# RWKV time mixing on one core: state steps moved by half a slot, the product with v moved into the next slot, zeros as fill on TensorE, and a rewritten drain

## The chip, the cores and the metric

The kernel runs on one core of a Trainium2 chip. The metric is the time of one execution on the device in microseconds; lower is better. The engines are called PE (TensorE, matrix multiply), DVE (VectorE), ACT (ScalarE), POOL (GpSimd) and SP (SyncE, which only issues transfers here).

## The reference

For each of 16 batches and 256 channels a recurrence runs over 2048 time steps. Its state is a weighted sum `aa` of values, a sum `bb` of weights and a running maximum `pp` that keeps the exponentials in range.

```python
for t in range(seq_len):
    ww = u + kk
    qq = np.maximum(pp, ww)
    e1 = np.exp(pp - qq)
    e2 = np.exp(ww - qq)
    output[b, t, :] = (e1 * aa + e2 * vv) / (e1 * bb + e2 + 1e-08)
    ww = pp - w + kk
    qq = np.maximum(ww, kk)
    e1 = np.exp(ww - qq)
    e2 = np.exp(kk - qq)
    aa = e1 * aa + e2 * vv
    bb = e1 * bb + e2
    pp = qq
```

Inputs and output are float32: k, v and the output have 33.55 MB each.

## The kernel before

Time is cut into 16 chunks of 128 steps (two halves of 64, one half in each half of the 128 partitions). A chunk of four batches is a tile of 128 partitions by 1024 numbers; there are 64 tiles for k, 64 for v and 64 for the output, 0.52 MB each. The main loop has one **slot** per tile (`n` from 0 to 63), and then 12 slots of drain. Four slots make one chunk of all 16 batches: a **period**; `n % 4` tells where in it a slot stands.

What happens to tile `n`, by the names in the code:

- `load_k`, `load_v`: six buffers each. k comes over SP's queue; v over SP's queue for the first 16 tiles and over POOL's queue after that.
- `round_k(n)` (L168) casts k to the format that PE multiplies, two slots ahead of use. DVE does it, except in slots with `n % 4` of 1 or 2 after slot 10, where POOL does.
- `logs(n)` (L196 and L200, the **exponents**): PE builds the decayed exponents, into two separate half tiles `xh` for the first nine tiles and into one tile `X` for the rest. Each has one buffer, so the exponents of tile n+1 wait for the exponentials of tile n.
- `exps(n)` (L206, L208): ACT takes the exponential and writes it into `EZR`, a ring of 12 tiles. In the first nine slots this goes in two halves.
- `cast_v(n)` (L215) casts v to bf16 into `vb`, which has two buffers; DVE or ACT does it for early tiles and POOL from tile 11 on. `times_v(n)` (L220) is the **product** with v on DVE, which stands at the end of slot n from slot 11 on.
- Ten slots later (`LAG`): `den` and `num` (L354), the sums over time by PE, each into a PSUM bank of its own with one buffer; `log_den` (L364, **logarithm**) and `invert` (L368, **inverse**) on ACT give 1/den as exp(-ln den); `mult` (L384, the **quotient**) on DVE multiplies and issues the store in three transfers on SP. The output tile `ot` has three buffers.
- `keep_going` (L360, the **fills**) multiplies zeros into the `den` tile, `DUM[n % 4]` times per slot. The logarithm of that tile waits for them.

Once per period the state is carried from chunk to chunk, in small **state steps**: `sums` (PE, 32 matmuls) and `copy_sums`, `turn` (PE) and `copy_turn` (tile `TS`), `state_logs` (ACT), `state_shift`, `state_frames` (a scan, L282) and `state_offsets` (DVE), a cap on POOL, `state_weights` (ACT, tile `G`), `state_chain` (the table product `TB`), `state_scan` (two scans, L309) and `state_spread` (DVE), `turn_back` (PE) and `inject`, which copies the carries and writes them over two ring rows of `EZR` by four small transfers, two on POOL's and two on SP's queue. They are queued in `later` by slot and by a name such as "frames"; the main loop takes each name up at its place.

Every instruction keeps the order in which the program writes it (`K`), so the main loop's text is the queue of each engine. Each engine takes its instructions in that order and waits where a tile isn't ready.

After tile 63's exponentials the exponent banks are freed and `den` and `num` get a second bank each (`drain`). There one of the three stores of a tile goes over POOL's queue, and the last tile's stores over SP and ACT.

Of the kernel before, what the change touches and what calls it, by code (L numbers as in the profile page):

```python
# [15 lines left out]
def kernel(  # L16
# [26 lines left out]
    DUM = (0, 4, 5, 3)  # L43
# [90 lines left out]
    def sum_matrices():  # L134
        OH = consts.tile([128, 56], BF16, tag="OH", name="OH")
        fill(OH, 0.0)
        for h in range(2):
            fill(OH[HS * h:HS * h + HS, 22 + h:23 + h], 1.0)
            fill(OH[HS * h:HS * h + 1, 30 + h:31 + h], 1.0)
        Sel = consts.tile([128, 3, 2, 2, 4, 2], F32, tag="Sel", name="Sel")  # L140
        fill(Sel, 0.0)
        for j, r in ((0, 64), (1, 0), (2, 8)):
            for h in range(2):
                select(Sel[:, j, h], NE, 1.0, -r - h, 1, [[-16, 2], [-2, 4], [-32, 2]])
        mats["OH"], mats["Sel"] = OH, Sel.rearrange("p a h x c i -> p (a h x c i)")
        Lx = matrix("Lx", F32)
        K(POOL.tensor_scalar(Lx, M1, -1.0, None, ALU.mult))
        for h in range(2):
            select(Lx, NE, 1.0, -(HS * h + HS - 1), 1, [[0, 128]])
        mats["Lx"] = Lx  # L150

# [71 lines left out]
    AS, D1, L1, A0, FR, _, BN = range(7)  # L223
    U_of = [consts.tile([128, 7, 32, 3], F32, tag=f"U{j}", name=f"U{j}") for j in range(2)]
    G_of = [consts.tile([128, 3, 32, 3], F32, tag=f"G{j}", name=f"G{j}") for j in range(2)]
# [5 lines left out]
    def state_start():  # L231
        for j in range(2):
            K(POOL.memset(CB_of[j], 0.0))
            K(POOL.memset(U_of[j][:, FR, :, 0:1], -BIG))
            K(POOL.memset(G_of[j][:, :, :, 0:1], 0.0))
        K(POOL.memset(U_of[0][:, D1, :, 0:1], -100.0))
        K(POOL.memset(U_of[0][:, L1, :, 0:1], 0.0))
        K(POOL.memset(TB_of[0][:, :, :, 0:1], 0.0))

    def sums(c):  # L240
        t = banks("num", "tot")[:, 0, 0:256]
# [16 lines left out]
    def turn(c):  # L258
        TS = banks("num", "TS")[:, 0, 0:192].rearrange("p (a x b m) -> p a x b m", a=6, x=2, b=2)
# [11 lines left out]
    def state_logs(c):  # L271
        K(SC.activation(U_of[c % 2][:, D1:D1 + 2, :, 1:3],
                        st[c, "TS"][:, 2:6, :].rearrange("p (a h) x -> p a x h", a=2), ACT.Ln))

# [9 lines left out]
    def state_offsets(c):  # L284
        U, nxt = U_of[c % 2], U_of[(c + 1) % 2]
        K(DVE.scalar_tensor_tensor(U[:, BN, :, 1:3], U[:, AS, :, 0:2], -1.0, U[:, FR, :, 1:3],
                                   op0=ALU.mult, op1=ALU.subtract))
        K(DVE.tensor_tensor(U[:, A0, :, 1:3], U[:, AS, :, 1:3], U[:, BN, :, 1:3], ALU.add))
        if drain:
            state_cap(c)  # L290
        if c + 1 < NST:
            K(POOL.tensor_copy(nxt[:, D1:D1 + 2, :, 0], U[:, AS:L1 + 1:2, :, 2]))  # L292

    def state_weights(c):
        K(SC.activation(G_of[c % 2][:, :, :, 1:3], U_of[c % 2][:, 0:7:3, :, 1:3], ACT.Exp, scale=-1.0))

    def state_cap(c):
        x = U_of[c % 2][:, BN, :, 1:3]
        K((DVE if drain else POOL).tensor_scalar(x, x, -CAP, None, ALU.max))
# [6 lines left out]
    def state_scan(c):  # L306
        G, TB = G_of[c % 2], TB_of[c % 2]
        for a in range(2):
            K(DVE.tensor_tensor_scan(AB[:, a].rearrange("p x h -> p (x h)"), G[:, 1].rearrange("p x h -> p (x h)"),  # L309
                                     TB[:, a].rearrange("p x h -> p (x h)"), 0.0, ALU.mult, ALU.add))  # L310

    def state_spread(c):
# [3 lines left out]
                         G[:, 2, :, 1:3].rearrange("p (b m) h -> p h b m", b=4).unsqueeze(1).broadcast_to([128, 2, 2, 4, 8])))  # L316
# [10 lines left out]

    def inject(c):
        if c == NST - 1:
            drain["carried"] = True  # L330
        cb = small.tile([128, 128], BF16, tag="cb", name="cb")
        K(DVE.tensor_copy(cb, st.pop((c, "CT"))))
# [29 lines left out]
    def log_den(n):  # L362
        rd = rpool.tile([128, 2, D], F32, tag="rd", name="rd")
# [11 lines left out]
    def mult(n):  # L375
# [4 lines left out]
        if last:  # L380
            for i in (1, 0):
                K(DVE.tensor_mul(oi[:, i], d[:, i], rd[:, i]))
        else:
            K(DVE.tensor_mul(oi, d, rd))  # L384
            K(SP.dma_start(out=dst[:, 0:2, :], in_=o[:, 0:2, :]))
        for h in range(2):
            K((POOL if drain and h and not last else SC if last and h else SP).dma_start(
                out=dst[HS * (1 - h):HS * (2 - h), 2:4, :], in_=o[HS * h:HS * h + HS, 2:4, :]))
        if last:
            for h in range(2):  # L390
                K((SP, SC)[h].dma_start(out=dst[HS * h:HS * h + HS, 0:2, :], in_=o[HS * h:HS * h + HS, 0:2, :]))
# [10 lines left out]
    for c in range(NST):  # L402
        s = 4 * c + 3
        if c == NST - 1:
            later[s, "last"] = [(sums, c), (copy_sums, c)]
            s -= 1
        for slot, where, f in ((s + 1, "sums", sums), (s + 1, "sums copy", copy_sums),
                               (s + 2, "turn", turn), (s + 2, "turn", copy_turn),
                               (s + 2, "logs", state_logs), (s + 2, "frames", state_shift),
                               (s + 2, "frames", state_frames), (s + 2, "frames", state_offsets),  # L410
# [119 lines left out]
```

## Time and profile before

| | |
|---|---|
| Runs (us) | 319.1, 316.5, 318.42; median 318.42 |
| Profiled execution | 319.99 us, of which the span is 318.3 us |
| Busy: PE, DVE, ACT, POOL | 254.9, 262.1, 259.7, 169.6 us (80, 82, 82, 53% of the span) |
| Bytes moved | 101.63 MB, mean 319 GB/s |
| Mean granted clock of PE | 0.922 |
| Transfers, issue to landing (median) | k 8.0 us, v on POOL's queue 7.2 us, stores 6.9 to 7.4 us, carries 5.5 to 5.9 us |

The page cuts the span into 40 slices of 7.96 us and gives tenths of busy time for each; PEclk is the clock that PE was granted, in tenths of full speed. A timeline row has start, duration (both us), engine, line, operation and tiles, and in brackets the idle time before it and what ended that. "SPq" and "POOLq" rows are transfers being issued. A row of the chain of waits has start, duration and what carried the time. A row of the groups has busy time in total and the mean duration of one in ns, then the idle time before them and its releaser.

Windows by stage, busy time in us of each engine (number of instructions in brackets left out):

| window, us | PE | DVE | ACT | POOL | PEclk | GB/s |
|---|---|---|---|---|---|---|
| 9.30 to 26.20 | 15.99 | 10.90 | 11.77 | 0.30 | 0.50 | 349 |
| 33.00 to 43.30 | 9.44 | 7.43 | 7.08 | 3.27 | 0.51 | 348 |
| 78.40 to 257.40 | 147.16 | 161.31 | 157.10 | 116.31 | 1.00 | 354 |
| 278.00 to 296.00 | 12.97 | 14.93 | 15.50 | 6.37 | 0.91 | 156 |
| 296.00 to 318.00 | 8.70 | 10.95 | 13.05 | 5.14 | 0.73 | 231 |

### The profile page before, as it was taken

Reading aid. Unit: us, or ns where it says so; the run is one execution under the profiler, and the core shown is the slowest. Engines: PE = TensorE matmul, PEld = TensorE weight load, DVE = VectorE, ACT = ScalarE, POOL = GpSimd, SP = SyncE. Lnnn points to the kernel's source line nnn. Section 1 sums busy time; section 2 is a strip of 40 time slices with the busy share of each in tenths; the row PEclk is TensorE's granted clock in tenths of the full one; section 3 lists DMA queues with packets and bytes.
Section 4 is the critical chain, followed back from the end, with each engine's and each line's share of the span. In section 5 each row is a group of like instructions: output and inputs, shape, how many; then the busy total and the mean of one; then the engine's idle time right before and its main releaser. Section 6 shows DMA issues by size and latency. Waiting matters only on the chain.

```text
span 318.3 us, 6417 instructions
## 1 busy us (share of the span) xinstructions
PE 254.9 (80%) x2324; PEld 127.7 (40%) x2351; DVE 262.1 (82%) x371; ACT 259.7 (82%) x244; POOL 169.6 (53%) x245
## 2 busy tenths in 40 slices
PE   7899887988788797788888797878788798975830
PEld 2334353444435344444434353434434354533310
DVE  4854768889898979989898889889898989898670
ACT  2665838988889889888889899888889889998880
POOL 5200136766574765766574765666574765432430
PEclk9556559999999999999999999999999999998695
DMA  7999999999999999999999999999999996646797
GB/s 191 356 348 349 348 337 347 344 385 297 321 348 359 358 296 334 382 373 390 361 374 305 381 332 379 339 346 360 357 373 338 373 352 202 169 120 169 206 273 203
DMA packets 86408, 101.63 MB, mean 319 GB/s; under 512 B 7068, under 2 KB 79848, under 8 KB 86376
## 3 DMA queue, kind: packets, MB, share of 16 engines
q1 hardware_dynamic: 77432, 73.91, 71.6%
q0 software_dynamic: 8640, 27.04, 25.1%
q8 instruction: 18, 0.29, 0.4%
q10 hardware_dynamic: 304, 0.27, 0.4%
q14 instruction: 14, 0.11, 0.1%
HBM read 67.12 MB, written 33.55 MB: 316 GB/s over the span
## 4 chain that ended last, share of the span: by engine, by line
DVE 27%; PE 24%; DMA 20%; ACT 15%; issue 7%; SPq 3%; POOL 1%; DVEq 0%; ACTq 0%; POOLq 0%
DMA out_dram<-ot 18%; DVE EZR L220 8%; ACT EZR L208 8%; DVE ot L384 7%; PE xh L200 6%; ACT rd L364 5%; PE X L200 5%; DVE AB L309 4%; PE xh L196 2%; PE num L354 2%; PE den L354 2%; PE TS L262 2%; ACT rd L368 2%; PE tot L247 2%; DMA kr<-in_k_dram 2%
## 5 line engine op out<-in xcount | busy, mean ns | idle before, releaser
L208 ACT ACTIVATE EZR<-X 128x2048 bf16<-128x2048 f32 x55 | 102.3, 1860 | 3.2 <-PE X L200 3.2
L220 DVE TENSOR_TENSOR EZR<-EZR,vb 128x2048 bf16<-128x2048 bf16 x64 | 88.9, 1389 | 8.3 <-ACT vb L213 6.0
L364 ACT ACTIVATE rd<-den 128x1024 f32<-128x1024 f32 x64 | 65.3, 1020 | 12.3 <-PE den L360 10.9
L215 POOL CAST vb<-vr 128x1024 bf16<-128x1024 f32 x53 | 55.0, 1038 | 36.2 <-DVE EZR L220 33.1
L368 ACT ACTIVATE rd<-rd 128x1024 f32<-128x1024 f32 x64 | 67.6, 1056 | 1.6
L384 DVE TENSOR_TENSOR ot<-num,rd 128x1024 f32<-128x1024 f32 x51 | 62.0, 1217 | 1.1 <-DMA out_dram<-ot 1.1
L68 POOL DMA_DIRECT2D vr<-in_v_dram x48 | 39.8, 829 | 15.1 <-POOL vb L215 10.4
L354 PE MATMUL num<-EZR,LN 64*64 64x512 bf16 x256 | 27.7, 403 | 22.9 <-DVE ot L384 19.1
L200 PE MATMUL X<-km,NLE 128*128 128x512 f32 x110 | 40.8, 452 | 0.8 <-POOL km L168 0.8
L360 PE MATMUL den<-Z 128*128 128x512 bf16 x138 | 36.6, 380 | 4.3 <-issue 4.3
L200 PE MATMUL X<-km,NLZ 128*128 128x512 f32 x110 | 35.0, 399 | 0.0
L196 PE MATMUL X<-WU,CO 32*128 32x512 bf16 x220 | 22.3, 390 | 15.1 <-ACT EZR L208 14.2
L292 POOL COPY U<-U 128x64 f32<-128x64 f32 x15 | 4.1, 276 | 52.5 <-DVE U L282 52.5
L168 DVE CAST km<-kr 128x1024 fp32r<-128x1024 f32 x39 | 30.2, 774 | 2.1 <-DMA kr<-in_k_dram 2.1
L196 PEld LDWEIGHTS <-CO 32*128 32x128 bf16 x256 | 11.4, 92 | 49.9 <-issue 47.3
L354 PE MATMUL den<-EZR,L 64*64 64x512 bf16 x256 | 28.2, 401 | 1.8 <-ACT rd L364 1.4
L354 PEld LDWEIGHTS <-LN 64*64 64x64 bf16 x256 | 13.2, 106 | 38.4 <-issue 33.8
L354 PE MATMUL num<-EZR,IdN 64*64 64x512 bf16 x256 | 27.6, 387 | 0.0
L354 PE MATMUL den<-EZR,Id 64*64 64x512 bf16 x256 | 27.2, 388 | 0.0
L309 DVE TENSOR_TENSOR_SCAN AB<-G,TB 128x96 f32<-128x96 f32 x32 | 26.5, 870 | 0.8
L168 POOL CAST km<-kr 128x1024 fp32r<-128x1024 f32 x25 | 26.2, 1049 | 0.1
L206 ACT ACTIVATE EZR<-xh 128x1024 bf16<-128x1024 f32 x18 | 18.2, 1019 | 8.4 <-PE xh L200 8.4
(76 smaller groups left out, 320.3 us busy)
## 6 DMA issues: line engine op xcount, KB each, us to landing
kr<-in_k_dram SPq DMA_DIRECT2D x64, 512.0 KB, 8.0
vr<-in_v_dram POOLq DMA_DIRECT2D x48, 512.0 KB, 7.2
out_dram<-ot SPq DMA_DIRECT2D x51, 256.0 KB, 7.4
out_dram<-ot SPq DMA_DIRECT2D x102, 128.0 KB, 6.9
vr<-in_v_dram SPq DMA_DIRECT2D x16, 512.0 KB, 8.8
out_dram<-od SPq DMA_DIRECT2D x12, 256.0 KB, 4.1
out_dram<-od SPq DMA_DIRECT2D x14, 128.0 KB, 3.7
out_dram<-od POOLq DMA_DIRECT2D x12, 128.0 KB, 3.4
```

Of the source, the lines that this page charges most:

```text
L68: K(q.dma_start(out=vr, in_=rows_of(v, n)))
L168: K(eng.tensor_copy(km, kr_of.pop(n)))
L196: K(PE.matmul(part_of(n, q)[:, i, :].rearrange("p (b d) -> p b d", b=2), CO[g:g + 32, :], WU[g:g + 32, :].unsqueeze(1).broadcast_to([32, 2 ...
L200: K(PE.matmul(part_of(n, q)[:, i, :], (NLE, NLZ)[q], km[:, i, :], start=False, stop=True, skip_group_check=True))
L208: K(SC.activation(ez(n)[:, 0:2], X_of[0], ACT.Exp))
L215: K(eng.tensor_copy(vb, vr_of.pop(n)))
L220: K(DVE.tensor_mul(ez(n)[:, 2:4], ez(n)[:, 0:2], vb.unsqueeze(1).broadcast_to([128, 2, 2, D])))
L309: K(DVE.tensor_tensor_scan(AB[:, a].rearrange("p x h -> p (x h)"), G[:, 1].rearrange("p x h -> p (x h)"), TB[:, a].rearrange("p x h -> p ( ...
L354: K(PE.matmul(d[x:x + HS, i, :], mats[m][r:r + HS, r:r + HS], ez(n)[r:r + HS, q, i, :], start=q == parts[0][1], stop=q == parts[1][1], til ...
L364: K(SC.activation(rd, DEN.pop(n), ACT.Ln, scale=RS))
L368: K(SC.activation(RD[n], RD[n], ACT.Exp, scale=-1.0))
L384: K(DVE.tensor_mul(oi, d, rd))
```

## The change

- **Start.** `state_start` sets its tables by memsets on DVE instead of POOL. In `sum_matrices` the order of two groups of set-up steps on POOL is exchanged.
- **Fills.** Slots 0 to 7 get three fills each, into a tile `pause` in the `den` bank. `DUM` goes from (0, 4, 5, 3) to (1, 1, 4, 4).
- **Product.** From slot 11 on the product of tile n moves from the end of slot n to the start of slot n+1, ahead of all else that DVE has there.
- **Casts of k** are all on DVE.
- **State steps.** Each moves later by about half a slot. `sums` and `turn` use the `den` bank instead of the `num` bank. The offsets become three steps (sum, a double difference, the cap), on POOL for chunks 2 to 14 and on DVE otherwise; the weights' exponential has 256 instead of 192 numbers per partition. The two scans become one of 192. The copy of the carries goes to ACT in most chunks.
- **Order in a slot.** The quotient comes after the product (and in slots with `n % 4` of 2 and 3 after the state steps); `num` stands ahead of `den` except where `n % 4` is 2.
- **Drain.** Slot 63 and the slots after it are written out by themselves (`ending`), with denominators two tiles ahead; `rd` takes `vr` buffers there; SP issues all stores, and the last tile's first half in one transfer.

```diff
-    DUM = (0, 4, 5, 3)
+    DUM = (1, 1, 4, 4)
...
     def state_start():
         for j in range(2):
-            K(POOL.memset(CB_of[j], 0.0))
+            K(DVE.memset(CB_of[j], 0.0))
...
     def sums(c):
-        t = banks("num", "tot")[:, 0, 0:256]
+        t = banks("den", "tot")[:, 0, 0:256]
...
+    def eng_of(c):
+        return DVE if c < 2 or c == NST - 1 else POOL
...
     def state_offsets(c):
-        U, nxt = U_of[c % 2], U_of[(c + 1) % 2]
-        K(DVE.scalar_tensor_tensor(U[:, BN, :, 1:3], U[:, AS, :, 0:2], -1.0, U[:, FR, :, 1:3],
-                                   op0=ALU.mult, op1=ALU.subtract))
-        K(DVE.tensor_tensor(U[:, A0, :, 1:3], U[:, AS, :, 1:3], U[:, BN, :, 1:3], ALU.add))
-        if drain:
-            state_cap(c)
+        U, nxt, e = U_of[c % 2], U_of[(c + 1) % 2], eng_of(c)
+        K(e.tensor_tensor(U[:, BC, :, 1:3], U[:, AS, :, 0:2], U[:, FR, :, 1:3], ALU.add))
+        K(e.tensor_tensor(U[:, A0:AA + 1:2, :, 1:3], U[:, AS, :, 1:3].unsqueeze(1).broadcast_to([128, 2, 32, 2]),
+                          U[:, BC, :, 1:3].unsqueeze(1).broadcast_to([128, 2, 32, 2]), ALU.subtract))
+        K(e.tensor_scalar(U[:, A2, :, 1:3], U[:, BC, :, 1:3], -1.0, -CAP, ALU.mult, ALU.max))
...
     def state_scan(c):
         G, TB = G_of[c % 2], TB_of[c % 2]
-        for a in range(2):
-            K(DVE.tensor_tensor_scan(AB[:, a].rearrange("p x h -> p (x h)"), G[:, 1].rearrange("p x h -> p (x h)"),
-                                     TB[:, a].rearrange("p x h -> p (x h)"), 0.0, ALU.mult, ALU.add))
+        K(DVE.tensor_tensor_scan(AB.rearrange("p a x h -> p (a x h)"), G[:, 1:3].rearrange("p a x h -> p (a x h)"),
+                                 TB.rearrange("p a x h -> p (a x h)"), 0.0, ALU.mult, ALU.add))
...
+    def copy_carries(c):
+        cb = small.tile([128, 128], BF16, tag="cb", name="cb")
+        if LAG < 4 * c + 7 < NP - 1:
+            K(SC.activation(cb, st.pop((c, "CT")), ACT.Copy))
+        else:
+            K(DVE.tensor_copy(cb, st.pop((c, "CT"))))
...
+    for n in range(NP):
+        q, kind = n - LAG, n % 4 if LAG < n < NP else -1
+        exps(n)
...
+        if LAG < n - 1 < NP - 1:
+            times_v(n - 1)
...
         if n + 1 < HALVES:
             logs(n + 1, (0,))
             logs(n + 1, (1,))
+            keep_going(psd.tile([128, 2, D], F32, tag="den", name="pause"), 3, True)
...
         if n >= LAG and n + 1 < NP:
             cast_v(n + 1, POOL)
+            if kind != 2:
+                next_v(n + 1)
+        if kind == 2:
+            small_work(n, "frames")
+        if kind == 3:
+            small_work(n, "chain")
+        if kind >= 0 and q >= 2:
+            mult(q - 2)
...
-        pooled = n > LAG and n % 4 in (1, 2)
-        if pooled and n + 2 < NP:
-            round_k(n + 2, POOL)
-            next_k(n + 2)
...
-        if LAG < n < NP:
-            times_v(n)
```

The steps of a chunk `c` (with `s = 4 * c + 3`), for all but the last chunk, by slot and place:

```diff
-        for slot, where, f in ((s + 1, "sums", sums), (s + 1, "sums copy", copy_sums),
-                               (s + 2, "turn", turn), (s + 2, "turn", copy_turn),
-                               (s + 2, "logs", state_logs), (s + 2, "frames", state_shift),
...
-                               (s + 3, "cap", state_cap), (s + 3, "weights", state_weights),
-                               (s + 3, "chain", state_chain),
...
+            plan = [(s + 1, "sums", sums), (s + 1, "sums", copy_sums), (s + 2, "turn", turn), (s + 2, "turn", copy_turn),
+                    (s + 3, "small", state_logs), (s + 3, "frames", state_shift), (s + 3, "frames", state_frames),
+                    (s + 3, "frames", state_offsets), ((s + 3, "late") if c > 1 else (s + 4, "small")) + (state_weights,),
+                    (s + 4, "chain", state_chain), (s + 4, "chain", state_scan), (s + 4, "chain", state_spread),
+                    (s + 4, "chain", state_keep), (s + 4, "turn back", turn_back), (s + 4, "back", copy_carries),
+                    (s + 4, "back", inject)]
```

## The prediction

> **What bounds the kernel now.** I read the page's strip of slices first, then the windows by stage, then the chain of waits and the timeline of each stage. A slot handles one pair tile of k and v; four slots are a period.
>
> ```profile
> PEclk9556559999999999999999999999999999998695
> DMA  7999999999999999999999999999999996646797
> ```
>
> Three stages show. From 9 to 47 us TensorE has half its clock nearly all the time; to 270 us all is steady; then the transfers thin out. Another row of the page gives 191 GB/s in the first slice and about 349 in the next four, where nearly everything is loads.
>
> The first stage, timeline and then chain of waits:
>
> ```profile
> 7.96 2.19 DVE L168 CAST km<-kr 128x1024 fp32r<-128x1024 f32 x1 [1.61 <-DMA kr<-in_k_dram]
> 8.00 0.53 POOL L233 MEMSET CB<- 128x512 bf16 x1
> ...
> 9.42 0.18 POOL L238 MEMSET TB<- 128x64 f32 x1
> 10.20 1.22 PE L200 MATMUL xh<-km,NLE 128*128 128x512 f32 x2 [1.24 <-DVE km L168]
> ```
>
> ```profile
> 18.72 1.15 PE xh L200 x2
> 19.88 0.54 PE xh L196 x2
> 20.41 1.15 PE xh L200 x2
> ```
>
> The cast of k tile 1 takes 2.19 us where its like takes 0.69: POOL's memsets hold it up to 9.6 us. TensorE stands still meanwhile, its clock falls at 9.3 us, and from there it is the chain without a gap, 2 x (0.54+1.15) = 3.38 us a slot.
>
> The steady stage, groups and then timeline:
>
> ```profile
> L208 ACT ACTIVATE EZR<-X 128x2048 bf16<-128x2048 f32 x55 | 102.3, 1860 | 3.2 <-PE X L200 3.2
> L364 ACT ACTIVATE rd<-den 128x1024 f32<-128x1024 f32 x64 | 65.3, 1020 | 12.3 <-PE den L360 10.9
> L368 ACT ACTIVATE rd<-rd 128x1024 f32<-128x1024 f32 x64 | 67.6, 1056 | 1.6
> ```
>
> ```profile
> 154.29 1.05 POOL L168 CAST km<-kr 128x1024 fp32r<-128x1024 f32 x1
> 154.31 2.12 DVE L220 TENSOR_TENSOR EZR<-EZR,vb 128x2048 bf16<-128x2048 bf16 x1
> 159.11 2.22 DVE L309 TENSOR_TENSOR_SCAN AB<-G,TB 128x96 f32<-128x96 f32 x2
> 160.06 1.05 POOL L168 CAST km<-kr 128x1024 fp32r<-128x1024 f32 x1
> ```
>
> Exponentials start at 78.40 (slot 17) and 257.44 us (slot 57): ten periods of 17.90 us. From start to start ScalarE needs 1.79 for exponentials, 1.05 for the logarithm (L364) and 0.97 for the inverse (L368), 3.81 a slot; with state logs 0.24 and weights 0.27 that is 15.8 a period, so 2.1 are stalls, of which 1.1 is the wait for the fills behind `den`. VectorE is as full (161.3 of those 179 us), but 2.5 us a period of it is blocking by POOL's casts of k: the product takes 2.12 for 1.21, the two scans 2.22 for 0.61.
>
> The drain:
>
> ```profile
> 308.82 1.48 SPq L385 DMA_DIRECT2D out_dram<-od  x1
> 310.34 0.60 SPq L387 DMA_DIRECT2D out_dram<-od  x1
> 311.04 1.45 SPq L385 DMA_DIRECT2D out_dram<-od  x1
> 312.53 1.91 SPq L387 DMA_DIRECT2D out_dram<-od  x2
> ```
>
> ScalarE does 11 pairs of 2.03 us; SyncE ends 4.4 us behind the last product at 310.7.
>
> **Start and clock.** The state's memsets move to VectorE behind that cast, which then ends at 8.65 instead of 10.15. They cost VectorE 1.2 us (two like the 0.27 of the Z memset, seven of about 0.1), done by 9.9, where the cast of v began anyway (10.07). So slot 1 starts 1.5 us sooner and TensorE keeps working through 9.3 us. Three fills of 128x512 per slot 0 to 7 cost 0.43 us each at half clock (ten in 4.45 us) and 0.22 at full (five in 1.25). With full clock a slot is 1.7 us of TensorE (the halves at 30 us: about 0.85) plus 0.7: no longer the bound. Slots 0 to 2 are then VectorE's, 0.60+1.15+0.62 = 2.4; slots 3 to 6 ScalarE's, 2 x 1.02 + 1.05 = 3.1; slots 7 and 8 about 2.8. From exponentials of slot 2 at 13.3: slot 3 15.6, slot 7 28.0, slot 9 33.6, with 0.8 for state work 34.4. Loads permit it: 1.5 MB in the first slice (191 GB/s), then 349 GB/s bring k tile 9, the 18th of 0.524 MB, at 30.7, so exponentials from 32.4. Before: 43.87. **-9.5 us.** Slots 9 and 10 at 3.9 instead of 4.4: **-1**. With the clock low all the way a slot is 3.38+1.28 = 4.66, and slot 9 begins at about 47.5: +3.6.
>
> Will the clock hold? I count 0.22 us of streaming for 512 columns, pairs on separate rows once. 29.6 to 33.0 us, after which it fell, has some 1.2 in 3.4: 35%. 143.0 to 146.4, the thinnest stretch I found in which it held, has 1.7 (exponents 1.3, carries 0.2, numerators 0.2): 50%. The new slot gives exponents 1.3 and fills 0.66 in 2.7 to 3.1 us: 63 to 73%. I take it as held. The Trainium skill, "TensorE: Matmul & The Clock Gate", Part 1, says that a sustained busy window of about 3.4 us releases the throttle and that it returns after an idle one. The two rises in this trace, at 29.6 and 46.7 us, lie five such windows apart, so the window agrees; but 9.3 to 26.2 us shows 15.99 of 16.90 us busy at clock 0.50, so plain busy time does not release it here. By the page alone the fills would add nothing to an engine that is 95% busy, and this term would be the 1.5 us of the start.
>
> **The steady period.** All k casts go to VectorE: +2 x 0.62. Off it go two offset steps (0.23+0.18), the cap was POOL's already, the carry copy (0.25), one scan (0.36 of 0.72; a scan twice as long was not run, so it saves 0 to 0.36). The 2.5 us of blocking by k casts go. What is late next: the product now opens the slot, POOL's cast of v starts as it ends (that is its release), and so falls on shift and scan in one slot and on the table product and scan in the next. A table product beside such a cast took 0.51 for 0.28 and ended 0.15 after it, so I count 0.9 of blocking for each. VectorE comes to 15.4+1.0, under ScalarE.
>
> ScalarE: 4 x 3.81 + 0.24 + weights 0.33 (256 elements for 192) + carry copy 0.2 = 16.0. Its waits, walked slot by slot:
>
> State slot (n%4 = 2). In the slot before, the copy of TS needs TensorE's exponents (1.91 to 3.36 after that slot's start) and TS itself (0.6); with the copy 0.28 and k's cast 0.60 VectorE is free at 4.9, which is about 1.0 into the state slot. Product to 2.2, POOL's cast to 3.2, the scan behind it to about 3.6. Three POOL steps follow, of which only the cap (0.37) was there before. One-input steps of this size took POOL 0.28 and 0.37, a copy 0.44; at 0.28 each the three take 0.85, with two inputs at double price 2.2; the nearest rows are 0.37 to 0.45, so 1.25. Weights start at 4.9, ScalarE was ready at 4.1 (1.79+0.24+1.05+0.97): 0.8 lost (0.4 to 1.75), and the next exponentials are queued behind. On POOL the load of v stands behind the offsets; it has about five slots until its use.
>
> Slots 3 and 0. In slot 3 VectorE does product (to 1.2 after the exponentials' start), table (1.5), waits for POOL's cast (2.6), scan and spread (3.3) and quotient (4.5); numerator, denominator and four fills follow to 6.5 while the logarithm could begin at 5.8: up to 0.7. If the scan is not blocked, that vanishes, and 0.2 comes up a slot later, where the denominator waits for the copy of the sums (now in its bank).
>
> The carries' four transfers follow ScalarE's copy, about 4.2 into slot 3, on POOL ahead of the next cast of v, on SyncE behind a k load. They landed in 5.5 to 5.9 us; the denominators that read them start some 11.5 after the same point. Before, the copy came at 4.8 (146.13 against 141.34), so that cover grows.
>
> So 17.0 to 17.5; I take 17.25. Ten periods save 6.5 us; with the POOL bounds 16.6 to 18.4, that is +5 to -13. **-6.5.**
>
> Transfers: a period moves 6.29 MB. The window 134 to 152 us ran 380 GB/s at share 1.07, which would allow 16.6; at 17.25 it is 365. Loads end near 268, 17 us ahead of the last product (285), and the gain eats this lead; I put **+1.5** for waits.
>
> **Drain.** The 11 pairs and two state steps are 23.0 of the 25.5 us from 283.95 to 309.40. The last carries still come late (logs a slot later), so I give 0.8 back. SyncE now has three issues a tile: 0.38+2x0.62 = 1.62 in quiet rows, under 2.03; but 2.8 and more by the late rows, which would be +8 over the tiles. If the transfers themselves set those rows, moving POOL's share costs nothing. I take +0.8. **0.** The order of setting up matrices, the rings for `rd` and fewer fills (10 a period for 12) I cost at nothing: POOL has them done by 8 us, `vr` buffers are free in the drain, and fills are cover only.
>
> Sum: 9.5+1+6.5-1.5 = 15.5 off 320.0 (the profiled run: span 318.3 and 1.7 around it; the median of the runs is 1.6 lower): 304.
>
> **Rivals.** *Clock not kept early* (17%): fills at 0.43 on the chain, 4.66 a slot. Against it the shares above, for it that even 95% busy did not raise it. +3.6-1-6.5 = -3.9: 316, 312 to 320.
> *POOL's offsets long* (12%): at 2.2 us ScalarE loses 1.75 and the period stays near 17.9, so only -9.5-1+1.5 is left: 311. For it: each step waits for the one before; against: the short rows.
> *SyncE bounds the drain* (10%): +8: 312. For it: SyncE has hardly a gap from 299.3 to 315.1; against it: quiet rows of 0.38 and 0.62.
> *No stalls* (8%): POOL's cast lets the scans through; the period is at the transfers' 16.6, 6.5 less than the forecast: 298.
> *Clock lost in the steady stage* (11%), the slower end: around the state slot TensorE waits for the quotient and for the late exponentials, and one stretch of 3.4 us holds exponents 1.3 and denominators 0.4: 1.7, the 50% that just held. Below that the next such stretch runs at half clock and each period pays 1.7 us: 13 x 1.7 = 22 on top: 326. Against it, the clock held through 240 us of such periods.
>
> **How the numbers follow.** Forecast 42%, 304, own range 297 to 310. For 8 in 10 I reach down past the case without stalls, by the 1.5 of waits and the two 0.8 of the drain, and up into the clock rival: 295 to 317. One per cent, what a measurement tells from no change, is 3.2 us: faster below 315.2 takes forecast, no stalls, offsets, SyncE and 4 of the clock's 17: 0.76. Within: 0.11, from the early clock. Slower: 0.11 and 0.02 of it, 0.13.
>
> **What would show it.** Right: TensorE's clock at 1.0 from 10 to 47 us and the first 128x2048 exponentials by 36; ScalarE waiting for POOL's offsets some 0.8 us a period; no k cast on POOL and scans of 1.0 to 1.6 us; period 17.0 to 17.5. Wrong: clock 0.5 in slots 1 to 8; a period at 17.9 with weights waiting 1.5; SyncE ending over 8 us after the last quotient; a clock dip in each period.

## The result, and the profile after

The changed kernel takes 328.19 us (median of four runs, 327.66 to 331.29); the kernel before, on the same chip, 317.70 (316.50 to 319.10). The ratio is 1.0344 (95% interval 1.0290 to 1.0399): slower, where the prediction said 304 and a range of 295 to 317. The profiled run is 328.14, its span 326.4. In the tables below, times are medians of all runs, and a ratio is formed without the runs that lie more than 1.5% above the kernel's fastest.

The page's strips of the changed kernel (40 equal slices: granted clock of TensorE, and transfers):

```profile
PEclk9999999979999999999999999999999999989875
DMA  6999999999999999999999999999999974436697
```

The half clock between 9 and 47 us is gone, as was forecast for the fills together with the moved memsets; every run that has the one has the other, so which of them did it is not shown. One slice near 70 us is at 0.7. It helped for a while. Start of the exponentials (L208) in both traces, and the difference:

| slot | before | after | difference |
|---|---|---|---|
| 9 | 43.87 | 37.20 | -6.7 |
| 10 | 48.85 | 40.69 | -8.2 |
| 17 | 78.40 | 75.80 | -2.6 |
| 57 | 257.44 | 259.57 | +2.1 |
| 63 | 282.07 | 287.58 | +5.5 |
| end of the last inverse | 309.40 | 315.54 | +6.1 |
| end of the span | 318.3 | 326.4 | +8.1 |

Read downwards, the gain of 8.2 shrinks by 5.6 between slots 10 and 17. Ten periods of 18.38 us for 17.90 cost 4.7, the last six slots 3.4, the drain 0.6, and the stores behind the last quotient 1.9 (9.5 us for 7.6).

Between slots 10 and 17, the chain of waits (start, duration, what; "DMA" is the time of a transfer):

```profile
46.06 0.29 DVE km L168
46.35 16.04 DMA vr<-in_v_dram
62.40 0.03 issue
62.42 0.02 POOLq L215
62.44 0.08 issue
62.52 1.04 POOL vb L215
63.56 0.72 POOL U L289
64.28 0.07 issue
64.35 1.06 POOL U L290
65.41 0.36 issue
65.77 0.44 POOL U L292
```

A load of v that SyncE issued at 46.35 us landed 16 us later; the transfers queued ahead of it are the likely reason. POOL's cast waited for it, and POOL's offset steps stand behind that cast: the state slot 14 took 7.5 us. One execution is not the whole picture here: in x7 and x11 below, whose programs are the same up to the drain, slot 14 took 5.9 and 6.5 us, and slot 17 began at 74.87 and 76.49.

A state slot of the steady stage, timeline (start, busy, engine, line; in brackets the idle time before and what ended it):

```profile
174.04 0.23 DVE L280 TENSOR_TENSOR U<-U 128x64 f32<-128x64 f32 x1
174.30 1.07 DVE L285 TENSOR_TENSOR_SCAN U<-U 128x96 f32<-128x96 f32 x1
175.30 1.19 DVE L393 TENSOR_TENSOR ot<-num,rd 128x1024 f32<-128x1024 f32 x1
175.46 0.31 POOL L289 TENSOR_TENSOR U<-U 128x64 f32<-128x64 f32 x1 [0.30 <-DVE U L285]
175.86 0.48 POOL L290 TENSOR_TENSOR U<-U 128x128 f32<-128x128 f32 x1
176.41 0.97 POOL L292 TENSOR_SCALAR U<-U 128x64 f32<-128x64 f32 x1
176.42 0.68 DVE L168 CAST km<-kr 128x1024 fp32r<-128x1024 f32 x1
177.41 0.43 ACT L297 ACTIVATE G<-U 128x256 f32<-128x256 f32 x1 [1.40 <-POOL U L292]
178.34 0.83 POOL L68 DMA_DIRECT2D vr<-in_v_dram  x1
178.58 2.08 DVE L306 TENSOR_TENSOR_SCAN AB<-G,TB 128x192 f32<-128x192 f32 x1
179.18 1.05 POOL L215 CAST vb<-vr 128x1024 bf16<-128x1024 f32 x1
```

Three things are to be seen. ScalarE stands still for 1.40 us before the weights (L297). The third offset step (L292) takes 0.97 us beside VectorE's cast of k; at 65.77 above it took 0.44, with nothing of VectorE's beside it. And the merged scan (L306) takes 2.08 us while POOL issues a load and casts; in the run x5 below it took 0.56. The third step's 0.95 to 0.97 us stands in all eleven steady periods of this trace. The waits of the whole run (us in total, times, longest):

```profile
ACT G L297 <- POOL U L292: 21.1, 13, 3.1
...
ACT rd L369 <- PE den L364: 8.9, 14, 1.7
```

That is 1.62 us a period for the weights (1.39 to 1.57 in the steady stage, 3.14 and 1.99 in slots 14 and 62), where the prediction had 0.8, and 0.64 for the logarithm behind the fills.

### The profile page after: what moved, and what is told of

Same layout as the page of the kernel before. It is cut to its first block, busy times and chain, and to the rows that moved or that the text cites. A ratio compares the mean times of both kernels' runs of the same rounds, so it can differ in the third digit from the quotient of the medians.

```text
span 326.4 us, 6396 instructions
## 1 busy us (share of the span) xinstructions
PE 251.1 (77%) x2348; PEld 123.3 (38%) x2348; DVE 268.2 (82%) x353; ACT 264.3 (81%) x256; POOL 157.8 (48%) x223
## 4 chain that ended last, share of the span: by engine, by line
DMA 24%; ACT 22%; PE 21%; DVE 18%; issue 6%; SPq 3%; POOL 2%; DVEq 0%; ACTq 0%; POOLq 0%
DMA out_dram<-ot 10%; ACT EZR L208 10%; DMA vr<-in_v_dram 8%; DVE ot L393 7%; DMA kr<-in_k_dram 6%; ACT rd L369 6%; PE X L200 4%; PE num L358 4%; PE den L364 4%; ACT rd L373 3%; PE tot L247 3%; PE den L358 3%; DVE EZR L220 3%; DVE AB L306 2%; DVE U L280 1%
## 5 line engine op out<-in xcount | busy, mean ns | idle before, releaser
L208 ACT ACTIVATE EZR<-X 128x2048 bf16<-128x2048 f32 x55 | 102.4, 1861 | 4.0 <-PE X L200 4.0
L220 DVE TENSOR_TENSOR EZR<-EZR,vb 128x2048 bf16<-128x2048 bf16 x64 | 78.5, 1227 | 3.9 <-ACT vb L213 2.7
L168 DVE CAST km<-kr 128x1024 fp32r<-128x1024 f32 x64 | 47.0, 734 | 2.6 <-DMA kr<-in_k_dram 2.6
L68 POOL DMA_DIRECT2D vr<-in_v_dram x48 | 37.7, 785 | 11.9 <-POOL vb L215 10.7
L364 PE MATMUL den<-Z 128*128 128x512 bf16 x138 | 39.2, 383 | 0.0
L341 POOL DMA_DIRECT2D EZR<-cb x36 | 20.5, 572 | 26.0 <-ACT cb L328 11.3
L358 PE MATMUL num<-EZR,IdN 64*64 64x512 bf16 x256 | 26.6, 392 | 0.0
L294 POOL COPY U<-U 128x64 f32<-128x64 f32 x15 | 11.6, 775 | 29.2 <-DVE U L285 28.4
L306 DVE TENSOR_TENSOR_SCAN AB<-G,TB 128x192 f32<-128x192 f32 x16 | 24.7, 1546 | 0.7
L364 PEld LDWEIGHTS <-Z 128*128 128x128 bf16 x162 | 12.8, 97 | 32.1 <-issue 24.5
L297 ACT ACTIVATE G<-U 128x256 f32<-128x256 f32 x16 | 6.8, 423 | 21.1 <-POOL U L292 21.1
```

Of the source, the lines that this page charges most:

```text
L68: K(q.dma_start(out=vr, in_=rows_of(v, n)))
L168: K(eng.tensor_copy(km, kr_of.pop(n)))
L208: K(SC.activation(ez(n)[:, 0:2], X_of[0], ACT.Exp))
L220: K(DVE.tensor_mul(ez(n)[:, 2:4], ez(n)[:, 0:2], vb.unsqueeze(1).broadcast_to([128, 2, 2, D])))
L358: K(PE.matmul(d[x:x + HS, i, :], mats[m][r:r + HS, r:r + HS], ez(n)[r:r + HS, q, i, :], start=q == parts[0][1], stop=q == parts[1][1], til ...
L364: K(PE.matmul(d[:, j % 2, :], Z[:, 0:128], Z, start=first, stop=True, skip_group_check=True))
```

## The experiments

| run | what | us (lowest to highest, runs) | ratio to before (95%) |
|---|---|---|---|
| changed kernel | | 328.19 (327.66 to 331.29, 4) | 1.0344 (1.0290 to 1.0399) |
| x1 | offset steps on VectorE | 326.00 (323.28 to 337.71, 4) | 1.0212 (1.0124 to 1.0300) |
| x2 | cast of v behind the first scan | 334.56 (332.79 to 337.47, 4) | 1.0518 (1.0432 to 1.0604) |
| x3 | cast of v behind both scans | 320.72 (317.14 to 324.32, 4) | none |
| x4 | ten early loads of v left out | 323.47 (1) | none |
| x5 | x1 and x3 | 320.99 (320.12 to 323.27, 10) | 1.0081 (1.0040 to 1.0122) |
| x6 | before with the new start | 317.50 (315.73 to 318.81, 10) | 0.9962 (0.9920 to 1.0004) |
| x7 | a store of each drain tile on POOL | 326.51 (324.57 to 327.28, 4) | 1.0221 (1.0154 to 1.0289) |
| x8 | x3 and x7 | 321.42 (314.90 to 325.76, 10) | 0.9993 (0.9911 to 1.0075) |
| x9 | half of the later loads of v left out | 327.08 (326.82 to 327.33, 2) | 1.0298 (1.0239 to 1.0357) |
| x10 | x3 and x9 | 311.07 (309.50 to 312.64, 2) | 0.9794 (0.9725 to 0.9863) |
| x11 | one store for a drain tile | 323.29 (322.49 to 324.63, 4) | 1.0183 (1.0139 to 1.0227) |
| x12 | x6, loads of v on POOL from tile 10 | 317.03 (315.48 to 318.78, 12) | 0.9987 (0.9959 to 1.0015) |
| x13 | third offset step on VectorE | 318.45 (316.46 to 323.94, 10) | 1.0005 (0.9967 to 1.0043) |
| x14 | x13, x3 and x7 | 318.59 (312.40 to 322.79, 12) | 0.9858 (0.9790 to 0.9926) |
| x15 | x13 and x7 | 317.66 (316.06 to 319.57, 12) | 0.9994 (0.9963 to 1.0024) |
| x16 | x15, third step ahead of the quotient | 323.09 (321.95 to 325.35, 6) | 1.0153 (1.0105 to 1.0200) |

**x1: the offset steps on VectorE.**

```diff
     def eng_of(c):
-        return DVE if c < 2 or c == NST - 1 else POOL
+        return DVE
```

> The changed kernel with the three offset steps on VectorE in every chunk. Theory A (the steady loss is ScalarE's weights behind POOL's three steps, 1.92 us from 175.46 to 177.38 in the state slot): the steps take about 0.7 us on VectorE, the weights' wait of 21.1 us in all falls under 6, the period from 18.4 to 17.2-17.7 us, the whole to 317-321 us. Theory B (VectorE or the transfers set the period and the weights' wait is only where it shows): the wait moves elsewhere, the period stays within 0.2 of 18.4 and the whole at 327-330.

The ratio fell from 1.034 to 1.021, less than the weights' wait alone would give. The profile was taken at a granted clock of 0.746 (337.71 us), so its lines can't be set beside the others, and where the rest went isn't read from it. Left open here; x5 and x13 take it up.

**x2 and x3: POOL's cast of v behind the scans.** In x2 the cast moves behind the state slot's shift, scan and offsets; in x3 also behind the table product, scan and spread of the slot after:

```diff
+        if kind == 2:
+            small_work(n, "frames")
+        if kind == 3:
+            small_work(n, "chain")
         if n >= LAG and n + 1 < NP:
             cast_v(n + 1, POOL)
             if kind != 2:
                 next_v(n + 1)
-        if kind == 2:
-            small_work(n, "frames")
-        if kind == 3:
-            small_work(n, "chain")
```

> The changed kernel with POOL's cast of v put behind the offsets in the state slot, so that shift, scan and offsets go first. Theory A: the scan falls from 1.07 to 0.36 us, the offsets begin 0.7 to 0.9 sooner, the weights' wait goes from 1.6 to 0.5-0.9 a period, the period to 17.5-17.8, the whole to 318-322 us. Theory B: no change beyond 0.2 us a period, 327-330.

> As the kernel before it, and POOL's cast of v also behind the table step in the next slot. If the cast alone blocks the long scan (2.08 us, 0.56 when nothing runs on POOL): scan 0.6, the quotient 1.4 us sooner, the wait of the logarithm for the fills in the slot after it (0.63) gone, period 16.8-17.2, whole 311-316. If the issue of a v load ahead of it blocks the scan too (178.34 to 179.17): scan about 1.0, period 17.0-17.5, 314-319. Theory B: 327-330.

x2 fell out the other way: the weights' wait went down to 8.7 us in all, but the time rose to 334.56. Its clock strip tells a part of why:

```profile
PEclk9999999979999899969969999999879699989975
```

TensorE lost its clock again and again in the steady stage: this is the rival "clock lost in the steady stage", in a neighbour of the changed kernel. There the spread (L311) took 2.04 us in ten of its sixteen turns, while POOL issued a load and cast, instead of 0.45, and ScalarE's copy of the carries waited 0.8 to 1.0 us in nine periods. Which of these starves TensorE enough isn't settled. The periods tell the two losses apart: four of the ten from 85.59 us on have the full clock and the long spread and take 18.4, as in the changed kernel, so the blocking had moved from the offsets to the spread; five have a mean clock of 0.84 to 0.91 and take 19.6 to 21.0; and the one whose spread took 0.45 (from 183.58 us) takes 16.99. x3 keeps the clock but for one slice, and five periods from 87.31 to 172.29 us are 17.0 each, inside the forecast. The second scan took neither of the two lengths expected: 1.27 us, beside the cast of v that had moved behind the offsets. Then its slots grow to 4.5 us. Windows before and after that point (PE, PEld, DVE, ACT and POOL busy us, then clock, DMA share and GB/s):

```profile
87.00:172.00 85.00, 73.89 (x732) 37.37 (x731) 77.24 (x96) 79.85 (x76) 56.42 (x76) 1.00 1.06 371
172.00:257.00 85.00, 72.18 (x710) 35.90 (x707) 73.84 (x92) 78.89 (x74) 50.66 (x71) 1.00 1.04 356
```

At 17.0 us a period asks for 370 GB/s, and in this run VectorE waits 12.2 us in all for an output buffer whose store has not landed. Whether the transfers are the cause is what x9 and x10 decide.

**x5: both remedies.**

> The changed kernel with the offset steps on VectorE (0.23 + 0.29 + 0.19 us a period more for it) and POOL's cast of v issued behind the scan of the frames in the state slot and behind the scan of the carries in the slot after. Nothing is left out of the computation. Theory A (the whole loss of the steady stage is the weights waiting for POOL's offset steps, plus blocked scans): the wait of the weights is under 0.3 us a period, both scans are at 0.36 and 0.56, periods about 17.0 until the transfers bind, time 312 to 317, and no faster than with the casts moved alone (320.7) by more than 5. Theory B (transfers of 6.29 MB a period at some 365 GB/s set 17.2 us whatever the engines do): periods start at 17.0 and come back to about 18 after 170 us, time 317 to 322, like the casts moved alone.

Theory A's waits came true (the weights' wait 2.4 us in all, scans of 0.36 and 0.56), its time did not: 320.99, periods of 17.5 but for two of 18.1 and 19.9. With the three steps in VectorE's queue the third is now the one that POOL's cast holds up (1.03 us for 0.19 in the steady periods), and the logarithm's wait for the fills grew to 22.1 us in all. The blocking moved rather than went away.

**x4: early loads left out.** Tiles 6 to 15 take the v of tile 5:

```diff
-            load_v(n + NBUF, SP if n + NBUF < FIRST else POOL)
+            if n + NBUF < FIRST:
+                vr_of[n + NBUF] = held[NBUF - 1]
+            else:
+                load_v(n + NBUF, POOL)
```

> The changed kernel, leaving out the loads of v for tiles 6 to 15, which use tile 5's v again (5.2 MB less to read). Theory C (the part of the early gain that is missing, 37.2 for 34.4 at slot 9 and 75.8 for about 69 at slot 17, went to transfers): slot 9 at 34-36, no wait for a v load at slot 14, slot 17 at 69-71.5, the whole 4-6 us shorter, period unchanged at 18.4. Theory D (engines set these slots): slot 9 within 0.7 of 37.2, slot 17 within 1 of 75.8.

Slot 9 starts at 37.23, as before the edit, so the loads of v from tile 6 on don't set that. Slot 17 starts at 73.17 instead of 75.80: some 2.6 of the 5.6 us that vanish between slots 10 and 17 go with those loads (1.7 to 3.3 beside the other executions of the same program, x7 and x11); the rest is there without them, in a state slot 14 that still takes 5.9 us (58.69 to 64.59), as state slots of the steady stage do (5.8).

**x6 and x12: the new start alone.** x6 is the kernel before with the memsets on VectorE, the selection matrix filled earlier, and

```diff
             logs(n + 1, (1,))
+            keep_going(psd.tile([128, 2, D], F32, tag="den", name="pause"), 3, True)
```

x12 adds `FIRST = 10` for 16.

> The kernel before with only the new start: the state's memsets on VectorE, the selection matrix filled earlier, and three fills of zeros in each of slots 0 to 7. Nothing is left out. If the early gain is real by itself: clock 1.0 from 10 us, slot 9's exponentials at 37 instead of 43.87, and the time 310 to 313 (-5 to -7). If the loads take it back (the wait for a load of v about slot 14, as in the changed kernel): slot 9 at 37, slot 17 at 74 to 76 instead of 78.4, time 314 to 316.

> The kernel before with the new start (317.5), and the loads of v from tile 10 on, instead of 16, issued by POOL, so that a store does not queue behind as many loads on SyncE's ring. Nothing is left out. If the early gain was lost only to the store that landed after 8.6 us behind queued loads: that wait is under 4 us, slot 17 at 73 to 75 instead of 77.5 and the time 312 to 315. If the sum of the bytes sets it: slot 17 at 77 again and 317.

x6 reaches slot 9 at 38.19, 5.7 us sooner, and slot 17 at 77.46, 0.9 sooner. Its chain of waits shows where the rest went:

```profile
58.96 1.93 SPq L385
60.89 0.05 issue
60.94 1.06 SPq L387
62.00 0.05 issue
62.05 8.60 DMA out_dram<-ot
70.69 0.04 issue
70.74 1.24 DVE ot L384
```

One of the first stores, queued behind the loads that run ahead, landed after 8.6 us, and the quotient waited for its buffer. Such a store stands at the same place in x3 (63.03, 7.03 us) and x13 (60.17, 9.28 us). In x12 it is gone from there, but slot 9 took 6.8 us and slot 17 starts at 76.83. Neither run is told from the kernel before. Slot 17 lies at 75.8 to 77.7 in the changed kernel, x3, x6, x12 and x13 whatever stalls on the way. This fits a place set by the bytes that have to be moved by then (348 GB/s with no gap from the second slice on). The soonest runs that move all of them are x16 (74.81) and x7 (74.87); those that move fewer come sooner still, x4 at 73.17, and x9 and x10 below at 73.44 and 72.11. That is no proof, and the engines' own stalls have a part in it.

**x9 and x10: transfers or engines in the steady stage.** Both leave out the loads of v for two of every four tiles from tile 19 on, x9 in the changed kernel and x10 in x3:

```diff
+            if n + NBUF > FIRST and n % 4 in (1, 2):
+                vr_of[n + NBUF] = held[n + NBUF - n % 4]
+            else:
-            load_v(n + NBUF, SP if n + NBUF < FIRST else POOL)
+                load_v(n + NBUF, SP if n + NBUF < FIRST else POOL)
```

> The changed kernel without the loads of v for two of every four tiles from tile 19 on (tiles 4m+3 and 4m+4 take the v of tile 4m+2): 5.24 MB a period for 6.29. It leaves that part of the input out, so its output is not the reference's. The loads that POOL issues in the state slot and the slot behind it stay. If engines alone set the changed kernel's steady period (weights behind POOL's offset steps): periods 18.2 to 18.4 as before (18.38), wait of the weights about 1.5 us a period. If transfers set it: 17.0 to 17.5.

> The same loads left out of the kernel with POOL's casts of v behind both scans (316.5 us of span, five periods of 17.0 and then 18 us). If its second half was held by transfers: 17.0 in all ten periods and the VectorE's wait for a store's buffer (12.2 us in all) under 3; span about 308 to 311. If something else sets in after 172 us: about 18 again there.

The pair decides. The changed kernel with a sixth of its bytes gone keeps its periods of 18.3 to 18.5, but for one of 19.5 (slots 21 and 57 start at 91.75 and 258.22: nine periods, 18.50 each) and its wait of 19.1 us for the weights: engines set it. x3 with the same bytes gone runs at 17.0 from end to end (98.77, 115.76, 132.75, 149.74, 166.73 and on to 251.63), its span is 307.8 for 316.5. Its windows:

```profile
87.00:172.00 85.00, 72.19 (x722) 37.17 (x731) 74.54 (x96) 80.02 (x76) 48.92 (x66) 1.00 0.98 315
172.00:257.00 85.00, 71.50 (x723) 37.41 (x730) 74.68 (x97) 79.88 (x76) 47.78 (x64) 1.00 0.94 302
```

ScalarE does as much in the second window as in the first, where x3 fell back, and the wait for output buffers is 1.9 us instead of 12.2. So the transfers, at share 1.06 and 371 GB/s, are the next bound right behind the engines, and cost 8.7 us of what x3 could give (the two spans).

**x13: the third step alone.** The step that scales and caps goes to VectorE, between the quotient and the cast of k:

```diff
         if kind >= 0 and q >= 2:
             mult(q - 2)
+        if kind == 2 and n // 4 - 1 > 1:
+            state_third(n // 4 - 1)
```

> The changed kernel with only the third of POOL's offset steps (scale and cap, 0.43 us alone, 0.97 beside VectorE's cast of k) put on VectorE, between the quotient and that cast; cast of v and order otherwise as changed. Nothing is left out. If VectorE's cast of k blocking that step is its share of the loss: the weights start some 0.6 us sooner, their wait falls from 1.5 to about 1.0 us a period, period 17.8, time 321 to 324. If the cast of v ahead of the steps holds them alone: wait 1.3 to 1.5, period 18.3, time 327 to 329.

It gave more than expected, 9.7 us by the medians. The state slot at 185.71 us, timeline:

```profile
189.25 0.31 POOL L289 TENSOR_TENSOR U<-U 128x64 f32<-128x64 f32 x1 [0.29 <-DVE U L285]
189.64 0.48 POOL L290 TENSOR_TENSOR U<-U 128x128 f32<-128x128 f32 x1
...
190.20 0.19 DVE L299 TENSOR_SCALAR U<-U 128x64 f32<-128x64 f32 x1
...
190.31 0.68 DVE L168 CAST km<-kr 128x1024 fp32r<-128x1024 f32 x1
...
190.48 0.43 ACT L302 ACTIVATE G<-U 128x256 f32<-128x256 f32 x1 [0.68 <-DVE U L299]
```

The weights start 0.10 us after the third step, and 4.77 us after the exponentials for 5.48 in the changed kernel. Their wait is 9.8 us in all (9.1 behind this step, 0.7 behind L290), 0.75 a period for 1.62; and the six periods from 103.20 to 208.35 are 17.52, for 18.38. The wait fell by 0.87 and these periods by 0.86; over all ten from slot 17 to 57 (76.08 to 252.48) a period is 17.64, 0.74 less, and VectorE's wait for output buffers has grown from 1.0 to 10.6 us. So in this order of steps the period follows the wait. It isn't the only term: x10 has the same wait (0.68) and periods of 17.0. The expectation had counted only the 0.54 of blocking, not the 0.43 of the step itself, which also left POOL's series.

**x16: the third step ahead of the quotient.**

```diff
+        if kind == 2 and n // 4 - 1 > 1:
+            state_third(n // 4 - 1)
         if kind >= 0 and q >= 2:
             mult(q - 2)
-        if kind == 2 and n // 4 - 1 > 1:
-            state_third(n // 4 - 1)
```

> The same with the third step ahead of the quotient in VectorE's queue. Nothing is left out. If the rest of the weights' wait (0.75 us a period) still sets the period: wait 0.3 to 0.4, periods of 17.1 to 17.2 where the transfers let them, time 312 to 315. If the transfers set it (at 17.5 they run at 359 GB/s): periods of 17.4 to 17.6 with longer waits for stores, time 316 to 318, as x15.

Neither happened. The wait for the weights fell to 0.45 us a period, and yet the periods came to 18.2 and the time to 323.09, 5.4 slower than x15. The chain of waits:

```profile
171.70 1.08 DVE U L285
...
172.86 0.32 POOL U L289
...
173.38 1.22 DVE ot L399
174.60 0.69 DVE km L168
175.29 1.13 DVE EZR L220
176.42 0.21 DVE TB L306
```

The chain now runs through VectorE: the third step waits for POOL's first (0.43 us at this place, 7.3 in all), and quotient, cast, product and table product queue behind it. The state slot is shorter (4.78 us), the one after it longer (4.98 for 3.98 in x13). VectorE is the other bound, half a microsecond away.

**x7 and x11: the drain's tail.** x7 gives POOL one of the three stores of each drain tile but the last, as before the change; x11 stores such a tile by one transfer of 512 KB, so the halves of two sequences land swapped:

```diff
-                K(SP.dma_start(
+                K((POOL if drain and h and not last else SP).dma_start(
```

```diff
+            if drain and not last:
+                if i == 0:
+                    K(SP.dma_start(out=dst, in_=o))
+                return
```

> The changed kernel with one of the three stores of each drain tile but the last issued by POOL again, as before the change. Nothing is left out. If SyncE's issuing sets the tail: the span ends 7.5 instead of 9.5 us after the last quotient, time 326 (-2). If the rate at which stores are written sets it (266 GB/s between 307 and 324 us): no change within 0.7, 328.

> The changed kernel with each drain tile but the last stored by one transfer of 512 KB instead of three (the rows of two sequences then land swapped in their halves; the bytes are the same). If SyncE's issuing sets the tail: the span ends about 7 us after the last quotient for 9.5, time 325 to 326. If the rate of writing sets it: 9 to 9.5, time 328.

The changed kernel's last issues:

```profile
313.91 1.27 SPq L390 DMA_DIRECT2D out_dram<-od  x2
315.27 0.54 SPq L388 DMA_DIRECT2D out_dram<-od  x1
315.57 1.29 DVE L396 TENSOR_TENSOR od<-num,rd 128x512 f32<-128x512 f32 x2 [0.77 <-ACT rd L373]
315.86 1.26 SPq L390 DMA_DIRECT2D out_dram<-od  x2
...
319.17 0.54 SPq L388 DMA_DIRECT2D out_dram<-od  x1
319.75 2.61 SPq L390 DMA_DIRECT2D out_dram<-od  x4
322.46 0.55 SPq L388 DMA_DIRECT2D out_dram<-od  x1
```

SyncE issues a tile every 1.95 us without a pause, and when the last quotient ends at 316.86 it still has some two tiles to go. Behind the last quotient the span ends after 9.5 us; in x7 after 7.9, in x11 after 5.1. With one transfer a tile the same bytes went at 340 GB/s in the next to last slice of the page, where the changed kernel shows 269. So issuing set the tail rather than the rate of writing: x7, with transfers of the same sizes, shows 1.6 us of it. x11 changes the size of the transfers as well as their number, so which of the two gave its further 2.8 us isn't told apart. By the ratios x11 is 1.6% under the changed kernel.

**x8, x14, x15: together.**

> The changed kernel with POOL's cast of v behind the scans (as in the run that gave 320.7) and the split stores of the drain. Nothing is left out. If the two effects add: 318 to 319 by theory SyncE, 320 to 321 if the rate of writing sets the tail.

> The third step on VectorE, POOL's casts of v behind both scans, and one store of each drain tile on POOL. Nothing is left out. If the engines' loss was the weights and the scans: no wait of the weights over 0.2 us, periods of 17.0 or less until transfers set in, both scans at 0.36 and 0.56 in most periods; the transfers then hold the body at about 17.5 on average: 315 to 319, at most 1% off the kernel before. If the removal of the wait lets the whole steady stage run at 17.0: 310 to 312.

> The third step on VectorE behind the quotient (318.45) and one store of each drain tile on POOL. Nothing is left out. If SyncE's issuing sets the tail it gains 1.5 to 2 there: 316.5 to 317, some 0.4% under the kernel before; if not, 318.4.

x8 gains nothing over x3. x14 scatters between 312.4 and 322.8; its ratio of 0.9858 rests on its two lowest runs of twelve, and its median of 318.59 is no better than x13's, so no gain is claimed. In its profiled run the quotient waited 23.0 us for stores, and the third step, queued behind the quotient, with it: 9.8 us of waiting for the weights are back, by way of the transfers. x15 is 317.66 beside 317.72 for the kernel before: the change mended in two places is no slower and no faster. No version that does the whole work is shown to beat the kernel before.

## The prediction, step by step

**The clock, right; the size of the start, too large.** The clock is full through the first slots and the exponentials of slot 9 came 6.7 us sooner, not 9.5; at 37.20 they missed the sign that was named, "by 36". Between 9.3 and 26.2 us TensorE was busy for 15.70 of 16.90 us at clock 1.00, where before it was 15.99 at 0.50, so the share of busy time doesn't tell the two states apart; whether the fills made the difference or the closing of the gap that the memsets had left stays open. Slot 3 began at 15.52, as reckoned (15.6); slots 3 to 6 took 14.3 us for 12.4, slots 7 and 8 took 7.4 for 6.4. The prediction had checked the loads of k alone, and ScalarE's cast of v tile 3 waited 0.64 us for its load, which landed at 18.07; the rest of the chain passes through work on TensorE that was taken as cover: three fills of a slot, 0.68 us, between two slots' exponents, and the first chunk's sums (1.06). Then the gain was lost: of 8.2 us at slot 10, 2.6 were left at slot 17. The prediction kept the whole 10.5 to the end, so this is its second largest miss (7.9 us), and its cause is shown only in part (x4, x6).

**The steady period, wrong, and this is the step that failed.** "At 0.28 each the three take 0.85, with two inputs at double price 2.2; the nearest rows are 0.37 to 0.45, so 1.25", and so "0.8 lost". The walk up to there was good: the first scan ended 3.44 us after the exponentials' start (reckoned: 3.6) and ScalarE was ready at 4.09 (4.1). The steps took 0.31, 0.48 and 0.97, with their gaps 1.92, and ScalarE lost 1.40 here and 1.62 on average. The period came to 18.38, the far end of the bounds that the prediction gave for POOL (16.6 to 18.4). The term was mis-sized because the rows it was taken from had no cast of k beside them, and the change itself put that cast on VectorE, right behind the quotient. The Trainium skill, "SBUF — State Buffer", section "Who interferes with whom", says that VectorE and GpSimd share a pair of ports as an exclusive lock, that copies, casts and `tensor_scalar` on VectorE can take it, and that the other engine then blocks for the whole instruction. The trace agrees: 0.97 us beside a cast of 0.68, 0.44 without; and the steps beside the quotient, which reads its numerator from PSUM, kept 0.31 and 0.48. x13 is the proof: with that step off POOL, and so neither blocked nor in POOL's series, the wait came to 0.75, the size that was forecast, six periods to 17.5, the upper end of the forecast, and the time fell by 9.7 us. Of the 11.3 us by which ten periods missed 17.25, 7.4 hang on this step (17.64 over the ten). The walk's other term came as reckoned: the logarithm behind the fills waited 0.64 for "up to 0.7". In x10, where the second scan ends 0.8 us sooner, the slot with `n % 4` of 0 takes 3.86 for 4.52 us and the next one 4.10 for 3.91, the 0.2 that was said to come up a slot later.

**What made the miss larger than the rival.** "POOL's offsets long" had the mechanism and nearly the size (1.75), and put the time at 311. It kept the early gain of 10.5 whole and the last six slots at no cost. But the last slots of the kernel before run at 3.84 us once loads thin out, while in the changed kernel the state slots there still take 5.8 and 6.4: +3.4.

**Transfers, +1.5, far too small for the schedule that was forecast.** x3 against x10: 8.7 us. In the changed kernel itself the term was not put to the test: without a sixth of the bytes (x9) its periods stay as they are. The prediction noted 380 GB/s in one window and took it as room; 371 GB/s is where five periods of 17.0 stood, and no kernel that moves all bytes held it through the steady stage. With x13 the steady term is nearly as forecast, and the time is still 318 and not 304.

**The drain.** The rival "SyncE bounds the drain" was right in kind, though its sign, "SyncE ending over 8 us after the last quotient", did not show: SyncE's last issue ended 6.2 us after it (4.4 before), and the span 9.5 (7.6). It was priced at 8 us in all; the tail cost 1.9 against the kernel before and 4.4 against one transfer a tile.

**Rivals that didn't happen here.** The clock held through the steady stage of the changed kernel, though x2 shows how near that was. The mean scans were 0.67 and 1.55 us, within the 1.0 to 1.6 that was named only for the second. The carries' transfers, whose cover was to grow, held TensorE up once, for 1.4 us in slot 10 (0.3 in all before). One scan for two, the rings and the order of setup show no wait that the kernel before didn't have.

## What to carry to other kernels

A step's price is that of its neighbours in the new order: list what the other engine runs at that moment, and when the change moves that work too, take no row in which it was elsewhere. Before adding up gains on engines, work out the rate of transfers that the faster schedule asks for, and give away all that lies above the rate that some long stretch of the trace has held. A gain at the start is only a gain if the queues behind it can move the bytes sooner.

## What the runs showed of the hardware

- A small step on GpSimd beside VectorE's cast of k took 0.97 us for 0.44; in slot 14 the first step took 0.74 beside that cast and the second 1.34 beside VectorE's product, whose inputs both lie in SBUF, for 0.31 and 0.48 beside the quotient.
- The scan of 192 on VectorE took 0.56 us alone, 1.27 beside a cast on GpSimd (x13) and 2.08 with the issue of a load ahead of that cast (178.34 to 179.17). An issue without a cast behind it did not slow it (0.56 at 68.53 us in the changed kernel), so why the issue ahead of a cast adds so much is open.
- One transfer of 512 KB a tile reached 340 GB/s in a slice of the drain, three transfers of 256, 128 and 128 KB 269; SyncE took 1.95 us to issue the three.
- A load queued at 46.35 us landed 16.04 us later, and stores at that stage 7.0 to 9.3 us after the end of their issue, against medians, from the issue, of 8.9 for such loads and 5.9 to 6.5 for stores.
- The clock of TensorE, which stayed at 0.50 with the engine 95% busy before the change, stayed at full speed (93% busy) with three fills in each of the first slots and the memsets moved; and moving one cast on POOL (x2) was enough to lose it in five of ten steady periods.
